# A two-layer decoder kernel: high and low input parts side by side in one tile, one 512-column product in place of two of 256

## The chip, the cores and the metric

The program runs on one core of one Trainium2 chip. The metric is the device time of one execution in microseconds (us); three runs of the kernel before took 2767.17 to 2772.16 us, with a median of 2768.21 us. A core has five engines with a queue each: TensorE (PE in the profile, with its weight loads as PEld), VectorE (DVE), ScalarE (ACT), GpSimd (POOL) and SyncE (SP, which here only issues DMAs). TensorE multiplies a stationary operand of 128x128 (the weights, loaded ahead of each product) by a moving operand of up to 512 columns and adds the result up in PSUM, which has eight banks of 128 x 512 float32.

## The reference, cut to what matters

All arithmetic is float32. 16 meta tokens stand ahead of 256 input tokens, so T = 272; D = 2048.

```
h = concat(meta, x)                                   # 272 x 2048
h = h + rwkv7_time_mix(rms_norm(h))                   # layer 0
h = h + swiglu(rms_norm(h))                           # layer 0, F = 5632
k, v = rms_norm_heads(n @ sb_w_k), n @ sb_w_v         # n = rms_norm(h), 272 tokens
q = rms_norm_heads(rms_norm(h) @ sb_w_q)              # layer 1
h = h + stick_breaking(q, k, v) @ sb_w_o
h = h + (silu(m @ w_gate) * (m @ w_up)) @ w_down      # m = rms_norm(h)
return h[:, 16:]
```

Only the last 256 tokens are returned. From the queries on, layer 1 therefore needs 256 tokens, everything before it 272.

## The kernel before, in words

Activations lie with features on the partitions: a tile is 128 features by 272 or 256 tokens. A projection from 2048 features is 16 steps k over input tiles, for each of its output tiles of 128 features, added up in one PSUM bank.

Float32 accuracy comes from a split. Every weight and every activation is cut into a high part (rounded to the `fp32r` type by ScalarE, `nc.scalar.copy`) and a low part (the rest, by VectorE). A step k is then three `fp32r` products into the same bank: high weights by high input, high weights by low input, low weights by high input (`mm3`, L193 to L201; `mm3k`, L187 to L191; `proj_steps`, L223 to L238, which yields between steps so that other work can be put between them). High and low input parts are two tiles (`split`, L240; `split_gain`, L250).

Weights come from HBM in pieces of 128x1024 (or 128x384 at the end of a w_down row) on SP's queue (`parts`, L154). ScalarE makes `whi` and VectorE `wlo` for four steps at a time (128x512); there are six buffers of each (`NWHL`), so the split can be at most six groups of four steps ahead of TensorE.

The program has these stages: a prologue (first norm, key projection, low-rank inputs), the time mix of 16 head pairs, `wo_first` (output projection), `ffn(0)`, keys and values in `attention`, 16 heads in `attn_head` with the query projection, `sb_w_o`, and `ffn(1)`. `ffn` runs in four quarters: 11 gate tiles and 11 up tiles of 16 steps each, whose scaled product is split into 11 input tiles, then 16 output tiles of `w_down` with 11 steps each. With 256 tokens there are 256 steps of the query projection, 256 of `sb_w_o`, 2 x 44 x 16 = 1408 of gate and up and 4 x 16 x 11 = 704 of down: 2624 steps in all, by three products each.

A finished gate or up bank is read by one VectorE instruction that multiplies it by the norm factor `rs` (L994, L1000; L1087 for queries). A finished `w_down` or `sb_w_o` bank is added to the residual tile `h` by one (L1006, L1076). In `ffn` the banks alternate between two pools of two (`mmbank`, L176), in the heads they come from one pool of two.

The order on each engine's queue is set when the program is built, by a scheduler that follows data dependencies and buffer release. On one engine the instructions run in that order; engines wait for one another by semaphores.

Of the kernel before, what the change touches and what calls it, by code (L numbers as in the profile page):

```python
# [123 lines left out]
class Builder:  # L124
# [68 lines left out]
    def mm3(self, out, w, acts, n0, n1):  # L193
        nc = self.nc
        nk = len(w)
        for k in range(nk):
            wh, wl = w[k]
            xh, xl = acts[k]
            nc.tensor.matmul(out, wh, xh[:, n0:n1], start=k == 0, stop=False)  # L199
            nc.tensor.matmul(out, wh, xl[:, n0:n1], start=False, stop=False)  # L200
            nc.tensor.matmul(out, wl, xh[:, n0:n1], start=False, stop=k == nk - 1)  # L201

    def proj(self, src, acts, nk=NK, m=128, n0=0, n1=T):
        w = self.weights(src, nk, m)
        ps = self.mmbank()
        out = ps[:m, :n1 - n0]
        self.mm3(out, w, acts, n0, n1)
        return out

    def proj_pair(self, srcs, acts, n0=0):  # L210

        parts = [self.parts(src, NK, 128) for src in srcs]
        out = [self.mmbank()[:, :T - n0] for _ in srcs]
        k = 0
        for ws in zip(*parts):
            for i in range(len(ws[0])):
                x = tuple(t[:, n0:] for t in acts[k])
                for o, w in zip(out, ws):
                    self.mm3k(o, w[i], x, k == 0, k == NK - 1)
                k += 1  # L220
        return out

    def proj_steps(self, src, acts, n0=0, step=None):  # L223
        nc = self.nc
        step = step or PSTEP
        w = self.weights(src, NK, 128)
        ps = self.mmbank()
        out = ps[:, :T - n0]
        for k in range(NK):
            wh, wl = w[k]  # L230
            xh, xl = acts[k]
            xh, xl = xh[:, n0:], xl[:, n0:]
            nc.tensor.matmul(out, wh, xh, start=k == 0, stop=False)  # L233
            nc.tensor.matmul(out, wh, xl, start=False, stop=False)  # L234
            nc.tensor.matmul(out, wl, xh, start=False, stop=k == NK - 1)  # L235
            if k % step == step - 1:
                yield 1
        return out  # L238

    def split(self, src, pool, tag):  # L240

        nc = self.nc
        n = src.shape[1]
        hi = pool.tile([128, T], F32R, name="hi", tag=tag)
        lo = pool.tile([128, T], F32R, name="lo", tag=tag)
        nc.scalar.copy(hi[:, :n], src)  # L246
        nc.vector.tensor_tensor(lo[:, :n], src, hi[:, :n].bitcast(F32), ALU.subtract)  # L247
        return hi, lo

    def split_gain(self, src, g, n0, tag):  # L250
        nc = self.nc
        hi = self.xs.tile([128, T], F32R, name="hi", tag=tag)
        lo = self.xs.tile([128, T], F32R, name="lo", tag=tag)
        nc.scalar.activation(hi[:, n0:], src[:, n0:], AF.Copy, scale=g)
        nc.vector.scalar_tensor_tensor(lo[:, n0:], src[:, n0:], g, hi[:, n0:].bitcast(F32),
                                       ALU.mult, ALU.subtract)
        return hi, lo


    def build(self):  # L260
        tc, nc = self.tc, self.nc
        with ExitStack() as ctx:
            cp = ctx.enter_context(tc.tile_pool(name="cp", bufs=1))
            self.xs = ctx.enter_context(tc.tile_pool(name="xs", bufs=32))
# [45 lines left out]
            with ExitStack() as c2:  # L310
# [4 lines left out]
                self.kr = c2.enter_context(tc.tile_pool(name="kr", bufs=32))  # L315
# [15 lines left out]
    def time_mix(self):  # L331
# [3 lines left out]
        hid = self.hid_ctx.enter_context(hid)  # L335
        self.kp = self.hid_ctx.enter_context(tc.tile_pool(name="kp", bufs=NK))
# [25 lines left out]
        for k in range(len(self.o), NK):  # L362
            self.o.append(self.split(self.oraw[k], self.xs, "xs1"))
        self.hid_ctx.close()

    def prologue(self, hid):
# [3 lines left out]
        with ExitStack() as ctx:  # L370
            x0 = ctx.enter_context(tc.tile_pool(name="x0", bufs=32))
            wx = ctx.enter_context(tc.tile_pool(name="wx", bufs=NWX))
            pt = ctx.enter_context(tc.tile_pool(name="pt", bufs=3))
            hn = [self.xs.tile([128, T + 1], F32, name="hn", tag="xs2") for _ in range(NK)]
            xx = [self.xs.tile([128, T], F32, name="xx", tag="xs2") for _ in range(NK)]
# [47 lines left out]
            def mix(i, k, pool, tag):  # L423
                x = pt.tile([128, T], F32, name="xi", tag="tmp")
                mixed(i, k, x)
                return self.split(x, pool, tag)
# [6 lines left out]
            for k in range(NK):  # L433
# [8 lines left out]
                xk.append(mix(2, k, x0, "xs0"))  # L442
# [31 lines left out]
            def rest():  # L474

                for i, name in ((1, "dec_w1"), (4, "a_w1")):
                    ps = self.psd.tile([128, 512], F32, name="lr", tag="sd")[:96, :T]
                    for k in range(NK):
# [3 lines left out]
                        x = self.xs.tile([128, T], F32, name="xi", tag="xs1")  # L482
# [11 lines left out]
                for k in range(KR):  # L494
                    self.xr.append(mix(0, k, self.xs, "xs2"))
                    yield 1
                x = []
                for k in range(NK):
                    x.append(mix(5, k, self.xs, "xs1"))
# [8 lines left out]
                for k in range(NK):  # L508
                    self.xv.append(mix(3, k, self.xs, "xs1"))
                    yield 1  # L510
                for k in range(KR, NK):
                    self.xr.append(mix(0, k, self.xs, "xs2"))
# [407 lines left out]
    def finish_h(self, k, n0, first, gains):  # L920
# [10 lines left out]
        return [self.split_gain(h, self.vec(g, k), n0, t) for g, t in gains]  # L931
# [7 lines left out]
    def wo_head(self):  # L939
# [4 lines left out]
        for k in range(KHEAD):  # L944
            while len(self.oraw) <= k:
                yield 1
            self.o.append(self.split(self.oraw[k], self.xs, "xs1"))
# [11 lines left out]
    def wo_first(self):  # L959
# [3 lines left out]
        for m in range(NK):  # L963
# [11 lines left out]
            acts.append(self.finish_h(m, 0, m == 0, [("g_ffn0", "xs2")])[0])  # L975
# [3 lines left out]
    def ffn(self, layer, n0):  # L979
        nc, a = self.nc, self.a  # L980
        n = T - n0
        gains = [("g_kv", "xs1"), ("g_mix1", "xs2")] if layer == 0 else None
# [205 lines left out]
```

## Time and profile before

| | |
|---|---|
| median of three runs | 2768.21 us |
| profiled execution | 2767.91 us, its span 2766.1 us |
| PE busy | 2713.5 us, 98% of the span |
| DVE busy | 1806.7 us, 65% |
| ACT busy | 1470.2 us, 53% |
| mean granted TensorE clock | 0.995 |
| DMA | 439.86 MB, mean 159 GB/s |

The span is the time from the first to the last recorded instruction; the profiled execution's own time is 1.8 us more. Products overlap in TensorE: a record of a product lasts some 280 ns, while the next one starts 0.12 us after it. What a product costs in a stream is therefore the distance between starts, or a stretch in which PE is busy throughout divided by its count of products, and not the mean duration of a row.

### The profile page before, as it was taken

To read this page: it belongs to the slowest core of one execution; us is meant where nothing else is said; L and a number is where in the kernel's file an instruction comes from. 1 tells how busy PE (TensorE), PEld (TensorE's weight loads), DVE (VectorE), ACT (ScalarE), POOL (GpSimd) and SP (SyncE) were. 2 spreads that over 40 slices of the span, in tenths; PEclk is the share of its full clock that TensorE was granted. 3 is DMA by queue.
4 is the path that set the end of the run, shared out by engine and by line. 5 is a ranking of instruction groups with operands and counts; after the bars stand their busy time and mean duration, and the time that the engine had idled before them with its cause. 6 is when DMAs were issued, how large, how long until landed. Compare 5 with 4: busy or idle time off the path is not lost.

```text
span 2766.1 us, 59131 instructions
## 1 busy us (share of the span) xinstructions
PE 2713.5 (98%) x23486; PEld 2610.8 (94%) x23486; DVE 1806.7 (65%) x3992; ACT 1470.2 (53%) x2901; POOL 1.2 (0%) x11
## 2 busy tenths in 40 slices
PE   6989999999999999999999999999999999999999
PEld 5888888888999999999999999999999999999999
DVE  7677787776765555555556876577666566565665
ACT  7764555554554444444445754577554454454443
POOL 0000000000000000000000000000000000000000
PEclk9999999999999999999999999999999999999999
DMA  5443333331755555555555545533555655655655
GB/s 177 138 137 99 102 95 102 102 95 49 232 174 171 176 180 162 187 174 163 188 174 164 185 161 171 172 108 110 189 183 174 200 183 176 199 184 175 198 175 178
DMA packets 181302, 439.86 MB, mean 159 GB/s; under 512 B 57984, under 2 KB 84000, under 8 KB 181024
## 3 DMA queue, kind: packets, MB, share of 16 engines
q1 hardware_dynamic: 137632, 428.56, 48.0%
q10 hardware_dynamic: 43392, 7.52, 1.4%
q8 instruction: 184, 3.01, 0.5%
q14 instruction: 94, 0.77, 0.1%
HBM read 430.27 MB, written 5.74 MB: 158 GB/s over the span
## 4 chain that ended last, share of the span: by engine, by line
PE 92%; DMA 3%; ACT 2%; DVE 2%; issue 1%; SPq 0%; ACTq 0%; POOLq 0%; POOL 0%; DVEq 0%
PE mm L199 23%; PE mm L200 23%; PE mm L201 23%; PE mm L234 3%; PE mm L233 3%; PE mm L235 3%; DMA raw<-w_k 1%; PE zb L835 1%; PE cb L890 1%; PE yb L818 1%; PE mm L189 1%; PE mm L191 1%; PE mm L190 1%; PE hms L1025 1%; PE wa L844 1%
## 5 line engine op out<-in xcount | busy, mean ns | idle before, releaser
L173 DVE TENSOR_TENSOR wlo<-raw,whi 128x512 fp32r<-128x512 f32 (+1 forms) x1596 | 1079.3, 680 | 712.4 <-ACT whi L172 687.0
L199 PE MATMUL mm<-hi,whi 128*128 128x272 f32 (+1 forms) x5328 | 1523.2, 286 | 1.2 <-DVE h L972 0.9
L172 ACT CAST whi<-raw 128x512 fp32r<-128x512 f32 (+1 forms) x1596 | 972.3, 611 | 1038.6 <-PE mm L200 901.2
L200 PE MATMUL mm<-lo,whi 128*128 128x272 f32 (+1 forms) x5328 | 1520.1, 285 | 0.0
L201 PE MATMUL mm<-hi,wlo 128*128 128x272 f32 (+1 forms) x5328 | 1516.4, 285 | 0.0
L199 PEld LDWEIGHTS mm<-hi,whi 128*128 128x128 f32 x5328 | 1002.3, 188 | 5.5 <-issue 2.6
L201 PEld LDWEIGHTS mm<-hi,wlo 128*128 128x128 f32 x5328 | 1003.9, 188 | 1.4 <-issue 0.9
L200 PEld LDWEIGHTS mm<-lo,whi 128*128 128x128 f32 x5328 | 1004.3, 188 | 0.8
L233 PE MATMUL mm<-hi,whi 128*128 128x272 f32 (+1 forms) x768 | 231.7, 302 | 0.0
L234 PE MATMUL mm<-lo,whi 128*128 128x272 f32 (+1 forms) x768 | 226.2, 295 | 0.0
L235 PE MATMUL mm<-hi,wlo 128*128 128x272 f32 (+1 forms) x768 | 225.5, 294 | 0.0
L234 PEld LDWEIGHTS mm<-lo,whi 128*128 128x128 f32 x768 | 145.4, 189 | 5.4 <-issue 2.3
L233 PEld LDWEIGHTS mm<-hi,whi 128*128 128x128 f32 x768 | 145.3, 189 | 5.1 <-issue 0.7
L235 PEld LDWEIGHTS mm<-hi,wlo 128*128 128x128 f32 x768 | 145.4, 189 | 4.7 <-issue 2.2
L189 PE MATMUL mm<-hi,whi 128*128 128x272 f32 (+1 forms) x208 | 60.9, 307 | 17.7 <-ACT hi L246 17.6
L190 PE MATMUL mm<-lo,whi 128*128 128x272 f32 (+1 forms) x208 | 62.9, 305 | 0.5 <-DVE lo L247 0.4
L191 PE MATMUL mm<-hi,wlo 128*128 128x272 f32 (+1 forms) x208 | 62.9, 306 | 0.0
L189 PEld LDWEIGHTS mm<-hi,whi 128*128 128x128 f32 x208 | 40.1, 200 | 20.8 <-ACT hi L246 19.7
L1006 DVE TENSOR_TENSOR h<-h,mm 128x272 f32<-128x272 f32 (+1 forms) x128 | 54.0, 422 | 6.3 <-PE mm L201 6.3
L994 DVE TENSOR_TENSOR t<-mm,rstd 128x272 f32<-128x272 f32 (+1 forms) x88 | 38.1, 433 | 19.4 <-PE mm L201 15.7
L1000 DVE TENSOR_TENSOR u<-mm,rstd 128x272 f32<-128x272 f32 (+1 forms) x88 | 38.1, 433 | 17.3 <-PE mm L201 15.6
L420 ACT ACTIVATE u<-hn,vecs 128x272 f32<-128x272 f32 x96 | 45.5, 516 | 4.5 <-DVE hn L439 4.5
(270 smaller groups left out, 2187.3 us busy)
## 6 DMA issues: line engine op xcount, KB each, us to landing
raw<-w_gate SPq DMA_DIRECT2D x176, 512.0 KB
raw<-w_up SPq DMA_DIRECT2D x176, 512.0 KB
raw<-w_down SPq DMA_DIRECT2D x128, 512.0 KB
raw<-w_down SPq DMA_DIRECT2D x128, 192.0 KB
raw<-w_k SPq DMA_DIRECT2D x32, 512.0 KB
raw<-w_v SPq DMA_DIRECT2D x32, 512.0 KB
raw<-w_r SPq DMA_DIRECT2D x32, 512.0 KB
raw<-w_o SPq DMA_DIRECT2D x32, 512.0 KB
```

What stands on the lines that cost most here:

```text
L172: nc.scalar.copy(hi, part)
L173: nc.vector.tensor_tensor(lo, part, hi.bitcast(F32), ALU.subtract)
L189: mm(out, w[0], x[0], start=first, stop=False)
L190: mm(out, w[0], x[1], start=False, stop=False)
L191: mm(out, w[1], x[0], start=False, stop=last)
L199: nc.tensor.matmul(out, wh, xh[:, n0:n1], start=k == 0, stop=False)
L200: nc.tensor.matmul(out, wh, xl[:, n0:n1], start=False, stop=False)
L201: nc.tensor.matmul(out, wl, xh[:, n0:n1], start=False, stop=k == nk - 1)
L233: nc.tensor.matmul(out, wh, xh, start=k == 0, stop=False)
L234: nc.tensor.matmul(out, wh, xl, start=False, stop=False)
L235: nc.tensor.matmul(out, wl, xh, start=False, stop=k == NK - 1)
L1006: nc.vector.tensor_tensor(h[:, n0:], h[:, n0:], ps, ALU.add)
```

## The change

An input that 256 tokens wide products will read gets its high and low part in one tile, high in columns 0 to 255 and low in columns 256 to 511 (`pair_tile`). `mm3k` tells the cases apart by the length of the input tuple: with two parts (272 tokens) the three products stay as they were; with a third entry, the whole pair, it issues two products. The first is low weights by high input, 256 columns, into the first half of the bank. The second is high weights by the pair, 512 columns, over the whole bank. The first half of the bank then holds the sum of two of the three partial results, the second half that of high weights by low input, and the two halves must be added when the bank is read.

`scaled` does this for gate, up and query banks: ScalarE copies the second half to SBUF, VectorE adds the first half to the copy, and VectorE multiplies by `rs`. `added` does it for `sb_w_o` and `w_down` banks: two VectorE additions to `h`, one for each half. The tile pools are regrouped to pairs: where 32 single tiles were, there are 16 tiles of twice the width. A key and a value tile share one too. The low-rank inputs `xi` of the prologue, single tiles, now take a pair tile each, 16 in place of 32.

```
     def mm3k(self, out, w, x, first, last):
         mm = self.nc.tensor.matmul
-        mm(out, w[0], x[0], start=first, stop=False)
-        mm(out, w[0], x[1], start=False, stop=False)
-        mm(out, w[1], x[0], start=False, stop=last)
+        if len(x) == 2:
+            mm(out, w[0], x[0], start=first, stop=False)
+            mm(out, w[0], x[1], start=False, stop=False)
+            mm(out, w[1], x[0], start=False, stop=last)
+            return
+        n = x[0].shape[1]
+        mm(out[:, :n], w[1], x[0], start=first, stop=False, skip_group_check=True)
+        mm(out, w[0], x[2], start=False, stop=last, skip_group_check=True)
+
+    def scaled(self, dst, out, rs):
+        V, n = self.nc.vector, dst.shape[1]
+        if out.shape[1] == n:
+            V.tensor_tensor(dst, out, rs, ALU.mult)
+            return
+        c = self.tp.tile([128, SEQ], F32, name="c", tag="half")
+        self.nc.scalar.copy(c, out[:, n:])
+        V.tensor_tensor(dst, out[:, :n], c, ALU.add)
+        V.tensor_tensor(dst, dst, rs, ALU.mult)
+
+    def added(self, h, out):
+        n = h.shape[1]
+        for c in range(0, out.shape[1], n):
+            self.nc.vector.tensor_tensor(h, h, out[:, c:c + n], ALU.add)
...
+    def pair_tile(self, pool, n):
+        t = pool.tile([128, 2 * T], F32R, name="hl", tag="hl")
+        x = (t[:, :n], t[:, n:2 * n])
+        return x if 2 * n > 512 else (*x, t[:, :2 * n])
...
-            self.xs = ctx.enter_context(tc.tile_pool(name="xs", bufs=32))
+            self.xs1 = ctx.enter_context(tc.tile_pool(name="xs1", bufs=NK))
...
-                        x = self.xs.tile([128, T], F32, name="xi", tag="xs1")
+                        x = self.xs1.tile([128, 2 * T], F32, name="xi", tag="hl")[:, :T]
...
-                nc.vector.tensor_tensor(t[:, :n], gp, rs, ALU.mult)
+                self.scaled(t[:, :n], gp, rs)
...
-                nc.vector.tensor_tensor(u[:, :n], up, rs, ALU.mult)
+                self.scaled(u[:, :n], up, rs)
...
-                nc.vector.tensor_tensor(h[:, n0:], h[:, n0:], ps, ALU.add)
+                self.added(h[:, n0:], ps)
```

TensorE's queue at the end of the last w_down tile of `ffn(1)`, before: two steps, each of an input high part `hi` and low part `lo` with the weights `whi` and `wlo` (the figures are buffer numbers).

```order
L199 MATMUL mm_36462<-hi_35513,whi_36458 128x256
L200 MATMUL mm_36462<-lo_35514,whi_36458 128x256
L201 MATMUL mm_36462<-hi_35513,wlo_36459 128x256
L199 MATMUL mm_36462<-hi_35662,whi_36458 128x256
L200 MATMUL mm_36462<-lo_35663,whi_36458 128x256
L201 MATMUL mm_36462<-hi_35662,wlo_36459 128x256
```

The same place after the change, three steps, with the pair tile `hl`; L196 reads its first half, L197 all of it.

```order
L196 MATMUL mm_33999<-hl_33106,wlo_33996 128x256
L197 MATMUL mm_33999<-hl_33106,whi_33995 128x512
L196 MATMUL mm_33999<-hl_33228,wlo_33996 128x256
L197 MATMUL mm_33999<-hl_33228,whi_33995 128x512
L196 MATMUL mm_33999<-hl_33350,wlo_33996 128x256
L197 MATMUL mm_33999<-hl_33350,whi_33995 128x512
```

Two products to a step stand where three stood, and the low weights are needed first.

VectorE's queue where the first quarter of `ffn(1)` goes from up to down, before: `u` is the last scaled up bank, `s` its product with the gate, `lo` the low part of the last down input, `h` the first residual tile, and `wlo` are weight splits for products to come.

```order
L1000 TENSOR_TENSOR u<-mm,rstd 128x256
L173 TENSOR_TENSOR wlo<-raw,whi 128x384
L1001 TENSOR_TENSOR s<-s,u 128x256
L247 TENSOR_TENSOR lo<-s,hi 128x256
L173 TENSOR_TENSOR wlo<-raw,whi 128x512 x2
L1006 TENSOR_TENSOR h<-h,mm 128x256
```

The same place after the change, where `c` is ScalarE's copy of the bank's second half.

```order
L207 TENSOR_TENSOR u<-mm,c 128x256
L173 TENSOR_TENSOR wlo<-raw,whi 128x384
L208 TENSOR_TENSOR u<-u,rstd 128x256
L1014 TENSOR_TENSOR s<-s,u 128x256
L173 TENSOR_TENSOR wlo<-raw,whi 128x512
L255 TENSOR_TENSOR hl<-s,hl 128x256
L173 TENSOR_TENSOR wlo<-raw,whi 128x512
L213 TENSOR_TENSOR h<-h,mm 128x256
L173 TENSOR_TENSOR wlo<-raw,whi 128x384
L213 TENSOR_TENSOR h<-h,mm 128x256
```

One more addition stands ahead of the last low part, a 128x512 weight split too, and the residual tile takes two additions.

ScalarE's queue at this place, before: `s` is the gate, `hi` the high part of the last down input, and the rest are weight casts.

```order
L996 ACTIVATE s<-t 128x256
L172 CAST whi<-raw 128x384
L172 CAST whi<-raw 128x512 x2
L172 CAST whi<-raw 128x384
L246 CAST hi<-s 128x256
L172 CAST whi<-raw 128x512 x2
```

The same after the change, with the copy `c` and the pair tile `hl`.

```order
L1009 ACTIVATE s<-t 128x256
L172 CAST whi<-raw 128x384
L172 CAST whi<-raw 128x512 x2
L206 COPY c<-mm 128x256
L172 CAST whi<-raw 128x384
L172 CAST whi<-raw 128x512
L254 CAST hl<-s 128x256
```

The copy and one more 128x512 weight cast stand ahead of the last high part.

## Rows read from the trace of the kernel before

**Rows 1.** The page: engine totals; the chain that ended last, by engine.

```profile
PE 2713.5 (98%) x23486; PEld 2610.8 (94%) x23486; DVE 1806.7 (65%) x3992; ACT 1470.2 (53%) x2901; POOL 1.2 (0%) x11
...
PE 92%; DMA 3%; ACT 2%; DVE 2%; issue 1%; SPq 0%; ACTq 0%; POOLq 0%; POOL 0%; DVEq 0%
```

**Rows 2.** Stretches: length, busy time (count) of each engine, granted clock, DMA share, GB/s.

```profile
0.00:200.00 200.00, 170.06 (x1152) 148.43 (x1154) 145.85 (x349) 143.71 (x328) 1.19 (x11) 0.98 0.50 156
200.00:700.00 500.00, 481.20 (x5610) 410.45 (x5610) 374.50 (x1347) 273.50 (x646) 0.00 (x0) 0.98 0.33 95
...
1784.00:1931.00 147.00, 147.00 (x1110) 139.28 (x1109) 111.66 (x232) 105.81 (x233) 0.00 (x0) 1.00 0.33 112
1931.00:2014.00 83.00, 82.87 (x700) 82.65 (x699) 58.48 (x108) 47.57 (x91) 0.00 (x0) 1.00 0.56 183
2014.00:2766.00 752.00, 748.95 (x6324) 748.69 (x6323) 449.32 (x783) 360.53 (x629) 0.00 (x0) 1.00 0.57 184
```

**Rows 3.** Waits of all engines: who waited for whom, us in total, times, longest.

```profile
ACT whi L172 <- PE mm L200: 901.2, 1161, 1.7
```

**Rows 4.** Products of 256 columns: count, busy us, mean ns, idle before.

```profile
L199 PE MATMUL mm<-hi,whi 128*128 128x256 f32 x2336 | 657.4, 281 | 0.0
...
L233 PE MATMUL mm<-hi,whi 128*128 128x256 f32 x256 | 75.8, 296 | 0.0
...
L189 PE MATMUL mm<-hi,whi 128*128 128x256 f32 x32 | 9.0, 281 | 0.0
```

**Rows 5.** Stretches of split products alone: 272 columns to 1500, 256 from 2018.

```profile
1100.00:1500.00 400.00, 400.00 (x3184) 400.00 (x3183) 230.54 (x394) 181.27 (x319) 0.00 (x0) 1.00 0.54 174
2100.00:2500.00 400.00, 400.00 (x3378) 400.00 (x3377) 241.44 (x418) 193.43 (x338) 0.00 (x0) 1.00 0.57 186
975.00:1100.00 125.00, 125.00 (x993) 125.00 (x992) 73.14 (x124) 58.30 (x104) 0.00 (x0) 1.00 0.52 172
909.00:970.00 61.00, 61.00 (x492) 61.00 (x491) 34.09 (x60) 26.22 (x45) 0.00 (x0) 1.00 0.57 185
2018.00:2136.00 118.00, 118.00 (x1000) 118.00 (x999) 73.06 (x126) 60.49 (x106) 0.00 (x0) 1.00 0.57 186
2141.00:2200.00 59.00, 59.00 (x503) 59.00 (x502) 33.70 (x61) 26.77 (x47) 0.00 (x0) 1.00 0.61 195
```

**Rows 6.** Timeline of TensorE in a head: start us, us, then the instruction.

```profile
1919.12 0.86 PE L1115 MATMUL lt<-lk,consts 128*128 128x416 f32 x2
1919.82 0.41 PE L1116 MATMUL lt<-lk,consts 128*128 128x144 f32 x2
1920.06 0.30 PE L1118 MATMUL lt<-lk,consts 128*128 128x32 f32 x2
```

**Rows 7.** VectorE and ScalarE groups of 256 columns: count, busy us, mean ns, idle.

```profile
L1006 DVE TENSOR_TENSOR h<-h,mm 128x256 f32<-128x256 f32 x64 | 26.5, 414 | 6.3 <-PE mm L201 6.3
...
L994 DVE TENSOR_TENSOR t<-mm,rstd 128x256 f32<-128x256 f32 x44 | 18.7, 425 | 7.7 <-PE mm L201 5.2 <-PE mm L191 1.0
...
L1131 ACT COPY o<-op 128x256 f32<-128x256 f32 x16 | 6.1, 378 | 1.5 <-PE op L1128 1.5
```

**Rows 8.** Timeline of VectorE from up to down, first quarter of ffn(1).

```profile
2137.81 0.42 DVE L1000 TENSOR_TENSOR u<-mm,rstd 128x256 f32<-128x256 f32 x1
2138.28 0.56 DVE L173 TENSOR_TENSOR wlo<-raw,whi 128x384 fp32r<-128x384 f32 x1
2138.76 0.42 DVE L1001 TENSOR_TENSOR s<-s,u 128x256 f32<-128x256 f32 x1
2139.65 0.42 DVE L247 TENSOR_TENSOR lo<-s,hi 128x256 fp32r<-128x256 f32 x1 [0.47 <-ACT hi L246]
2140.17 0.69 DVE L173 TENSOR_TENSOR wlo<-raw,whi 128x512 fp32r<-128x512 f32 x1
```

**Rows 9.** Timeline of the same place on ScalarE.

```profile
2139.21 0.41 ACT L246 CAST hi<-s 128x256 fp32r<-128x256 f32 x1 [0.96 <-DVE s L1001]
2139.52 0.62 ACT L172 CAST whi<-raw 128x512 fp32r<-128x512 f32 x1
```

**Rows 10.** Timeline of the end of the program.

```profile
2762.67 0.28 PE L201 MATMUL mm<-hi,wlo 128*128 128x256 f32 x1
2762.98 0.42 DVE L1006 TENSOR_TENSOR h<-h,mm 128x256 f32<-128x256 f32 x1 [3.44 <-PE mm L201]
2763.43 0.33 SPq L1014 DMA_DIRECT2D outT<-h  x1
```

More of the change, by code (lines that the diff above doesn't have):

```diff
@@ L188, in mm3k, with proj, proj_pair @@
         mm = self.nc.tensor.matmul
[L189 to L207 removed]
+        if len(x) == 2:
[19 more added lines that the diff above has]
+            self.nc.vector.tensor_tensor(h, h, out[:, c:c + n], ALU.add)
+    def proj(self, src, acts, nk=NK, m=128):
+        w = self.weights(src, nk, m)
+        out = self.mmbank()[:m, :acts[0][-1].shape[1]]
+        for k in range(nk):
+            self.mm3k(out, w[k], acts[k], k == 0, k == nk - 1)
         return out
[L210 removed]
+    def proj_pair(self, srcs, acts):
         parts = [self.parts(src, NK, 128) for src in srcs]
[L213 removed]
+        out = [self.mmbank()[:, :acts[0][-1].shape[1]] for _ in srcs]
         k = 0
@@ L216, in proj_pair, with proj_steps @@
             for i in range(len(ws[0])):
-                x = tuple(t[:, n0:] for t in acts[k])
                 for o, w in zip(out, ws):
-                    self.mm3k(o, w[i], x, k == 0, k == NK - 1)
+                    self.mm3k(o, w[i], acts[k], k == 0, k == NK - 1)
                 k += 1
         return out
-    def proj_steps(self, src, acts, n0=0, step=None):
-        nc = self.nc
+    def proj_steps(self, src, acts, step=None):
         step = step or PSTEP
         w = self.weights(src, NK, 128)
-        ps = self.mmbank()
-        out = ps[:, :T - n0]
+        out = self.mmbank()[:, :acts[0][-1].shape[1]]
         for k in range(NK):
[L230 to L235, printed above, removed]
+            self.mm3k(out, w[k], acts[k], k == 0, k == NK - 1)
             if k % step == step - 1:
@@ L238, in proj_steps, with split, split_gain @@
         return out
-    def split(self, src, pool, tag):
-        nc = self.nc
[L243 to L250, printed above, removed]
-        nc = self.nc
[L252 to L257, printed above, removed]
+    def pair_tile(self, pool, n):
+        t = pool.tile([128, 2 * T], F32R, name="hl", tag="hl")
+        x = (t[:, :n], t[:, n:2 * n])
+        return x if 2 * n > 512 else (*x, t[:, :2 * n])
+    def split(self, src, pool):
+        nc = self.nc
+        x = self.pair_tile(pool, src.shape[1])
+        nc.scalar.copy(x[0], src)
+        nc.vector.tensor_tensor(x[1], src, x[0].bitcast(F32), ALU.subtract)
+        return x
+    def split_gain(self, src, g, pool):
+        nc = self.nc
+        x = self.pair_tile(pool, src.shape[1])
+        nc.scalar.activation(x[0], src, AF.Copy, scale=g)
+        nc.vector.scalar_tensor_tensor(x[1], src, g, x[0].bitcast(F32), ALU.mult, ALU.subtract)
+        return x
     def build(self):
@@ L421, in mixed, with mix @@
                 V.scalar_tensor_tensor(out, hn[k][:, 1:], self.vec(f"om{i}", k), u, ALU.mult, ALU.add)
-            def mix(i, k, pool, tag):
+            def mix(i, k, pool):
                 x = pt.tile([128, T], F32, name="xi", tag="tmp")
                 mixed(i, k, x)
-                return self.split(x, pool, tag)
+                if pool is not self.xs2:
+                    return self.split(x, pool)
+                hi, lo = (pool.tile([128, T], F32R, name=n, tag="s") for n in ("hi", "lo"))
+                A.copy(hi, x)
+                V.tensor_tensor(lo, x, hi.bitcast(F32), ALU.subtract)
+                return hi, lo
             ps = [(self.pmm if m < 2 else self.pfr).tile([128, 512], F32, name="mm",
@@ L946, in wo_head @@
                 yield 1
-            self.o.append(self.split(self.oraw[k], self.xs, "xs1"))
+            self.o.append(self.split(self.oraw[k], self.xs1))
             yield 1
@@ L1132, in attn_head @@
         self.dump("ao", m, o)
-        os[m] = self.split(o, self.xs, "xs1")
+        os[m] = self.split(o, self.xs1)
 def blocks(w, m=128):
```

58 lines of the change are left out of this document (30 added, 28 removed).

## The prediction

> **What bounds the kernel now.** I read the totals first, then the chain, then stretches stage by stage. TensorE is busy for 98% of the span and is 92% of the chain that ended last [rows 1], so a change is worth what it takes off TensorE's queue, or puts between its instructions. By stages the idle time lies in the first 700 us (29.9 and 18.8 us), while from the heads on there is next to none: 0.1 us in the 83 us of the output projection and 3.1 us in the 752 us of the second feed-forward, nearly all of it at the very end [rows 2]. All that the change is about lies in this full part. Over the whole run ScalarE waits 901.2 us for TensorE to release a weight buffer [rows 3]: the weight splits run as far ahead as their six buffers let them, so neither they nor the weight DMAs set the pace. In the second feed-forward VectorE is busy 60% (449.3 of 752) and ScalarE 48% (360.5) [rows 2].
>
> **Products removed.** The steps with 256 tokens are counted in three groups: 2336, 256 and 32, together 2624 [rows 4]. Each loses one of its three instructions, and none of its columns: 3 x 256 before, 256 + 512 after. So everything hangs on what a product costs beyond its columns. In a stretch of nothing but such products one takes 400/3378 = 118.4 ns at 256 columns, and 400/3184 = 125.6 ns at 272 [rows 5]. The granted clock is 1.00 there, the 2.4 GHz level, so 256 columns at one per cycle are 106.7 ns and 272 are 113.3. What is left is 11.7 ns and 12.3 ns. No row has an `fp32r` product of 512 columns; its cost is bounded from both sides:
>
> - If the excess belongs to the instruction (its start, its weight load), the wide product takes 213.3 + 11.7 = 225.0 ns, and a step saves 11.7 ns: 2624 x 11.7 = 30.7 us.
> - If it belongs to the columns, the wide product is twice the narrow one, 236.8 ns, and nothing is saved. A line through the two widths, (125.6 - 118.4)/16 = 0.45 ns a column, is near this end: 118.4 + 256 x 0.45 = 233.6 ns, 3.2 ns a step, 8.4 us.
> - If the excess is a weight load that a long product hides altogether, the wide one takes little over 213.3 ns. The nearest rows are the plain float32 passes of a head: 416 columns start 0.70 us ahead of the next group and are two passes, 350 ns each against 2 x 416/2.4 = 346.7; two passes of 144 columns take 0.24 us, 120 each against 120 [rows 6]. With 3 ns of excess the wide product is 216 ns and a step saves 21 ns, 55 us.
>
> The two widths tell the first two apart weakly, since they differ by 16 columns: 6.67 ns at one column per cycle, 7.40 if all is proportional (118.4/16). The long stretches say 7.2. The matched stages say 61/492 - 59/503 = 124.0 - 117.3 = 6.7 for w_down, and 125/993 - 118/1000 = 125.9 - 118.0 = 7.9 for gate and up [rows 5]. Stages of one width differ by as much as the question does, so I cannot settle it from here. I take the first: the same excess on two widths is what a cost per instruction looks like, and the w_down pair, where the streams are most alike, lies on it. 30.7 us.
>
> One rule of the notes on the chip speaks against this. The Trainium skill, "TensorE: Matmul & The Clock Gate", section "Back-to-back issue gap", gives a warm product N/2.4 + 2.5 ns. By it 256 columns take 109 ns where the trace has 118.4, so it does not hold for these products as it stands; but if its 2.5 ns are all that is fixed here too, the change saves only 2624 x 2.5 = 6.6 us, which is close to the line through the widths and is weighed there.
>
> **Work added behind a bank.** A gate, up or query bank (44 + 44 + 16 = 104) costs ScalarE a copy of 378 ns and VectorE one more instruction of about 425 ns; a w_down or output bank (64 + 16 = 80) costs VectorE one more addition of 414 ns [rows 7]. In the second feed-forward that is 88 x 0.425 + 64 x 0.414 = 64 us on VectorE and 88 x 0.378 = 33 us on ScalarE. VectorE comes to 513 of some 725 us, 71%, ScalarE to 394, 54%. The cover is the lead of the weight splits: six groups of four steps, 6 x 4 x 3 x 118.4 ns = 8.5 us ahead, against about 1.3 us by which the copy and additions hold up the splits queued behind them. Banks come free 0.4 to 0.8 us later, with three others in turn in the feed-forward. I take nothing. Uncovered, it is 104 x (0.378 + 0.425) + 80 x 0.414 = 117 us, the upper end. Going below nothing is excluded: no instruction leaves these two engines.
>
> In the heads the query's way lengthens by the same 0.8 us, with output, score and next-query products of other heads in TensorE's order before anyone needs it; TensorE is busy for 147 of 147 us there [rows 2]. Nothing; at worst 16 x 0.8 = 13 us.
>
> **Low weights first.** The first product of a step now needs `wlo`, which comes after `whi`. With 8.5 us of lead this costs nothing, at worst one split of 0.69 us [rows 8] at a place where the lead is gone.
>
> **The four turns from up to down.** Here the added work has no lead. Before, the last up bank is scaled at 2137.81 and the last low part is done at 2139.65 + 0.42 = 2140.07 [rows 8]. It is needed at the eleventh step of the first down bank, 10 x 3 x 118.4 ns = 3.55 us after the first, about 2141.3: 1.2 us to spare. Now the copy (0.38) and an addition (0.42) come first, and in VectorE's queue a 128x512 split (0.69) stands ahead of the low part, of which 0.47 falls into a wait that is there anyway [rows 8]; ScalarE has one more cast of 0.62 ahead of the high part [rows 9]. So 2140.07 + 0.80 + 0.22 = 2141.1 at the least, and with the cast 2141.7, while the wide steps bring the need forward to 2141.2. That is 0 to 0.5 us late at each of four turns, 0 to 2 us; I take 1.0.
>
> **The end.** The last bank is added and stored: product 2762.67, addition 2762.98 of 0.42, store at 2763.43 [rows 10]. A second addition makes it 0.4 us later.
>
> **Pools.** The low-rank inputs of the prologue get 16 buffers in place of 32, and the scheduler orders the first 700 us slightly otherwise. TensorE's idle time there is 48.7 us [rows 2]; a tenth of that either way, 5 us, is my estimate of what a different order may move. I take nothing.
>
> **Sum.** -30.7 + 1.0 + 0.4 = -29.3 us. The profiled execution took 2767.9 us (span 2766.1 and 1.8 around it) and lies 0.3 below the median of the runs, so 2768.2 - 29.3 = 2739 us. With the excess at 10.6 to 11.7 ns (117.3 and 118.4 less 106.7), 5 us for the pools, and the turns between their ends, this case reaches from 2733 to 2748.
>
> **Rivals.**
>
> *The excess goes with the columns.* The `fp32r` stream takes one column per cycle, the plain passes one in two, and these show almost no excess though each has its weight load too [rows 6]: this speaks for a stream that is simply fed a little too slowly, as do the slopes of 7.2 and 7.9 [rows 5]. Against it is the slope of 6.7, and that a weight load may hide in a slow pass and not in a fast one. By the line through the widths: -8.4 + 1.4 = -7, 2761; between 2756 and 2770.
>
> *The excess is the weight load, and a long product hides it.* For it: one product fewer has a load in its shadow, and the float32 passes hide theirs. Against it: an excess from the load alone should shrink from 256 to 272 columns, and it grew. -55 + 1.4, 2715.
>
> *The hand-over of banks becomes the wait.* Copy, addition and multiplication stand in order on two engines, and the splits are queued behind them; if the lead is used up in every tile, TensorE waits at each bank. For it: VectorE at 71%, and a copy that waits for TensorE at ScalarE's head. Against it: 901 us of waiting on TensorE [rows 3]. It decides from 29 of the 117 us on, a quarter of what is added; with half exposed it is 2739 + 58 = 2797.
>
> **How the numbers follow.** Chances: per instruction 50%, with the columns 33%, hidden load 6%, hand-over 11%. A change under 0.2%, 5.5 us, is about what a measurement of this kernel cannot tell from none. Faster: all of the first and third, 14 of the 33 of the second: 0.70. Slower: 8 of the 11 of the last and 2 of the second: 0.10. The same: 0.20. The range holds the first case and most of the second: 2733 to 2767, leaving out the hidden load, the hand-over and the far end of the columns.
>
> **What would show it.** In the stretch of the second feed-forward, a step (one L196 and one L197) should take 343 ns where three products took 355; 352 says columns, 334 a hidden load. ScalarE should still wait for TensorE at the weight casts. Idle time of TensorE before L196 with VectorE's `wlo` or `hl` as releaser, other than at the turns, would show the last rival. The stages before the heads should take the same time within 5 us; if they don't, the pools count, and the forecast is wrong by that much.

## The result and the profile after

The changed kernel takes 2741.3 us, median of four runs (2737.1 to 2746.7), against 2769.0 for the kernel before: a ratio of 0.9905, interval 0.9891 to 0.9918. That is 27.6 us less, and 2.3 us above the forecast. The span of the profiled execution is 2740.0 us, 26.1 less than before.

The totals and the chain of the page answer to [rows 1].

```profile
PE 2689.3 (98%) x20862; PEld 2475.0 (90%) x20862; DVE 1864.8 (68%) x4176; ACT 1493.5 (55%) x3005; POOL 1.2 (0%) x11
...
PE 91%; DVE 3%; DMA 3%; ACT 2%; ACTq 1%; issue 0%; SPq 0%; DVEq 0%
```

2624 instructions are gone from TensorE, just the number of steps [rows 4], but its share of the span is what it was, and of the chain it has 91% where it had 92%. VectorE and ScalarE have gained 58 and 23 us of work.

The stretches (columns as in [rows 2]): the first 700 us, a stretch of 272 columns, one of 256 and 512, and the whole second feed-forward.

```profile
0.00:200.00 200.00, 171.97 (x1162) 150.72 (x1163) 145.97 (x349) 144.33 (x330) 1.19 (x11) 0.97 0.50 156
200.00:700.00 500.00, 481.23 (x5684) 413.57 (x5684) 386.39 (x1370) 278.96 (x661) 0.00 (x0) 0.98 0.35 101
...
1100.00:1500.00 400.00, 400.00 (x3193) 400.00 (x3192) 232.53 (x399) 182.89 (x322) 0.00 (x0) 1.00 0.56 176
2100.00:2500.00 400.00, 400.00 (x2289) 350.28 (x2289) 270.57 (x510) 209.36 (x392) 0.00 (x0) 1.00 0.59 186
1998.70:2740.00 741.30, 737.39 (x4215) 645.30 (x4214) 496.26 (x935) 383.45 (x717) 0.00 (x0) 1.00 0.59 187
```

The fourth row holds the size that was in dispute. 400/2289 = 174.75 ns a product and two of them to a step are 349.5 ns, where three took 3 x 118.4 = 355.2 [rows 5]. A step saves 5.7 ns in this stretch, and not 11.7. The second row says where the rest came from: in the same 500 us of the first part there are 74 more TensorE instructions than before [rows 2], at the same busy time, in a part where the products did not change.

Each stage ends with a norm whose product `ms` waits for the last residual tile, so its start marks the stage. Of before:

```profile
774.50 0.70 PE L936 MATMUL ms<-sqacc,consts 128*128 128x272 f32 x2
...
1571.53 0.50 PE L936 MATMUL ms<-sqacc,consts 128*128 128x272 f32 x1
...
2013.81 0.45 PE L936 MATMUL ms<-sqacc,consts 128*128 128x256 f32 x1
```

And of after:

```profile
763.46 0.73 PE L949 MATMUL ms<-sqacc,consts 128*128 128x272 f32 x2
...
1558.79 0.50 PE L949 MATMUL ms<-sqacc,consts 128*128 128x272 f32 x1
...
1998.70 0.44 PE L949 MATMUL ms<-sqacc,consts 128*128 128x256 f32 x1
```

| stage | before, us | after, us | difference |
|---|---|---|---|
| prologue and time mix, to the first norm | 774.5 | 763.5 | -11.0 |
| first feed-forward | 797.0 | 795.3 | -1.7 |
| keys and values, heads, output projection | 442.3 | 439.9 | -2.4 |
| second feed-forward, to the end | 752.3 | 741.3 | -11.0 |

So the stages with changed products gave 13.4 us, and 11 came from a part whose products did not change. The first feed-forward has no 512-column product, and still its 1.7 us are not the spread between executions: in eight traces of kernels with pair tiles (the change and the experiments below up to the stride of 14) this stage takes 795.3 us each time. Its inputs, too, lie in pair tiles now; why that makes it shorter is not shown.

### The profile page after: what moved, and what is told of

Its sections match the earlier page's. It is cut to its first block, busy times and chain, and to the rows that moved or that the text cites. A ratio compares the mean times of both kernels' runs of the same rounds, so it can differ in the third digit from the quotient of the medians.

```text
span 2740.0 us, 53870 instructions
## 1 busy us (share of the span) xinstructions
PE 2689.3 (98%) x20862; PEld 2475.0 (90%) x20862; DVE 1864.8 (68%) x4176; ACT 1493.5 (55%) x3005; POOL 1.2 (0%) x11
## 4 chain that ended last, share of the span: by engine, by line
PE 91%; DVE 3%; DMA 3%; ACT 2%; ACTq 1%; issue 0%; SPq 0%; DVEq 0%
PE mm L197 22%; PE mm L191 16%; PE mm L193 16%; PE mm L192 15%; PE mm L196 11%; DMA raw<-w_k 1%; PE cb L903 1%; PE yb L831 1%; PE rm L871 1%; PE zb L848 1%; PE hms L1038 1%; PE cb L896 1%; PE z L1115 1%; DVE G L721 0%; PE ba L715 0%
## 5 line engine op out<-in xcount | busy, mean ns | idle before, releaser
L191 PE MATMUL mm<-hl,whi 128*128 128x272 f32 x3424 | 996.9, 292 | 19.4 <-ACT hl L254 18.5
L193 PE MATMUL mm<-hl,wlo 128*128 128x272 f32 x3424 | 995.9, 291 | 0.0
L192 PE MATMUL mm<-hl,whi 128*128 128x272 f32 x3424 | 991.4, 290 | 0.4 <-DVE hl L255 0.3
L197 PE MATMUL mm<-hl,whi 128*128 128x512 f32 x2624 | 919.8, 395 | 0.0
L196 PE MATMUL mm<-hl,wlo 128*128 128x256 f32 x2624 | 740.6, 282 | 0.0
L191 PEld LDWEIGHTS mm<-hl,whi 128*128 128x128 f32 x3424 | 645.8, 189 | 27.7 <-ACT hl L254 20.5
L192 PEld LDWEIGHTS mm<-hl,whi 128*128 128x128 f32 x3424 | 652.6, 191 | 4.2 <-DVE hl L255 1.3
L193 PEld LDWEIGHTS mm<-hl,wlo 128*128 128x128 f32 x3424 | 647.9, 189 | 4.8 <-issue 1.8
L197 PEld LDWEIGHTS mm<-hl,whi 128*128 128x128 f32 x2624 | 492.5, 188 | 112.7
L196 PEld LDWEIGHTS mm<-hl,wlo 128*128 128x128 f32 x2624 | 494.3, 188 | 0.6
L213 DVE TENSOR_TENSOR h<-h,mm 128x256 f32<-128x256 f32 (+1 forms) x224 | 93.9, 420 | 6.6 <-PE mm L197 6.0
L193 PEld LDWEIGHTS mm<-hi,wlo 128*128 128x128 f32 x256 | 48.8, 191 | 2.9 <-issue 2.4
L191 PEld LDWEIGHTS mm<-hi,whi 128*128 128x128 f32 x256 | 48.9, 191 | 2.4
L192 PEld LDWEIGHTS mm<-lo,whi 128*128 128x128 f32 x256 | 48.9, 191 | 1.0
```

What stands on the lines that cost most here:

```text
L196: mm(out[:, :n], w[1], x[0], start=first, stop=False, skip_group_check=True)
L197: mm(out, w[0], x[2], start=False, stop=last, skip_group_check=True)
L213: self.nc.vector.tensor_tensor(h, h, out[:, c:c + n], ALU.add)
```

## The experiments

Each ratio and gain below is against executions of the kernel before that were made beside the experiment's (medians 2767.3 to 2769.3 us).

The first question is which part of the change earned which part of the time. Theory: the wide product earns what it saves at about 5 ns a step, and the pair tiles of the pool `xs1`, which holds the low-rank inputs, earn the first 11 us by the order that they lead the scheduler to. Rival: all of it is the products, and the first part differs by chance.

**Pools alone.** All pools and pair tiles of the change, but three products to a step:

```diff
-        x = (t[:, :n], t[:, n:2 * n])
-        return x if 2 * n > 512 else (*x, t[:, :2 * n])
+        return t[:, :n], t[:, n:2 * n]
```

> The pair tiles and all pools of the change, but three products of 256 columns to a step and the old single read of a bank. Theory of the prediction (the gain is one instruction less per step, pools move nothing): no gain, 2764 to 2774 us, the norm product of the first feed-forward still starts at about 774 us. Theory of the new trace (about 11 us come from another order of TensorE's queue in the time mix, which the pair tiles bring about): 2756 to 2759 us, that product at 763 to 764 us, and the second feed-forward as long as before, 752 us.

Measured: 2757.6, ratio 0.9964 (0.9951 to 0.9976), so 9.7 us faster with not one product fewer. The first `ms` and the one that ends the first feed-forward, then a stretch of the second feed-forward and the whole of it:

```profile
762.66 0.50 PE L948 MATMUL ms<-sqacc,consts 128*128 128x272 f32 x1
1557.99 0.50 PE L948 MATMUL ms<-sqacc,consts 128*128 128x272 f32 x1
```

```profile
2100.00:2500.00 400.00, 400.00 (x3369) 400.00 (x3368) 241.21 (x417) 192.57 (x337) 0.00 (x0) 1.00 0.57 184
2000.76:2755.80 755.04, 751.90 (x6324) 751.64 (x6324) 450.35 (x783) 359.91 (x629) 0.00 (x0) 1.00 0.57 183
```

The first norm comes 11.8 us earlier than before, and a product takes 118.7 ns, where it took 118.4. What I had set at nothing, the pools, is worth more than a third of the gain. One thing I had not expected: the pair tiles alone make the second feed-forward 2.8 us longer (755.1 against 752.3), as they make the first 1.7 us shorter. From there the wide product saves 13.8 us in the second feed-forward, and not only 11.0.

**Products alone.** The wide products, with all of the pool `xs1`, the low-rank inputs among it, in single tiles (the output projection, which uses the same pool, keeps three products; 2368 of the 2624 steps are wide). TensorE's order in the first part is then that of before, product by product in the two traces.

```diff
+        if pool is self.xs1:
+            hi, lo = (pool.tile([128, T], F32R, name=x, tag="hl") for x in ("hi", "lo"))
+            return hi[:, :n], lo[:, :n]
...
-            self.xs1 = ctx.enter_context(tc.tile_pool(name="xs1", bufs=NK))
+            self.xs1 = ctx.enter_context(tc.tile_pool(name="xs1", bufs=2 * NK))
```

> The change, but the pool xs1 keeps high and low parts in single tiles as before, 32 of them; the output projection of the heads then stays at three products, so 2368 of 2624 steps are wide. TensorE's order up to the first feed-forward is then that of the kernel before. Theory of the prediction: 90% of the gain stays, 2742 to 2745 us. Theory of the new trace (a step saves about 5 ns, the rest is the order): 2368 x 4.9 ns = 11.6 us, 2756 to 2759 us, the norm product at about 774 us and the second feed-forward at 741 us.

Measured: 2756.0, ratio 0.9955 (0.9941 to 0.9969), 11.3 us faster. First `ms` and stretch:

```profile
780.54 0.50 PE L952 MATMUL ms<-sqacc,consts 128*128 128x272 f32 x1
```

```profile
2100.00:2500.00 400.00, 400.00 (x2289) 350.17 (x2288) 270.48 (x508) 210.38 (x394) 0.00 (x0) 1.00 0.60 188
```

The step is that of after, 349.5 ns, and the gain of the first part is gone with the order: this execution's `ms` is even 6 us later than before. (It was the slowest of its five, 4.4 above their median, and the time that the granted clock cost, added up in slices of 15 us up to `ms` (a slice times the share that was not granted), is 20.7 us here, 13.5 in before, 13.8 in after and 11.7 in the run with the pools alone. Less that time, the first `ms` stands at 759.8 here, 761.0 in before, 749.7 in after and 751.0 with the pools alone: the two with single tiles and the two with pairs lie some 10 us apart. In the four other traces with TensorE's order of after it starts at 760.6 to 763.5.) The two halves add up to 21.0 us of the 27.6. The 256 steps left out are 1.4 more, and 2.8 is what the wide product saves beyond its 11.0 once the tiles are pairs; the rest is within the intervals of three comparisons, some 3.5 us to either side of each.

**What a product costs by its width.** Other widths: 384 columns with the high weights and 128 with the low ones in the query, gate, up and output steps, 448 and 192 in the down steps, so 512 and 640 columns to a step. Parts of the sums are left out (fewer columns of the low weights' product, and only the first half of each bank is read).

```diff
-        mm(out[:, :n], w[1], x[0], start=first, stop=False, skip_group_check=True)
-        mm(out, w[0], x[2], start=False, stop=last, skip_group_check=True)
+        a, b = self.widths
+        mm(out[:, :b], w[0], x[2][:, :b], start=first, stop=False, skip_group_check=True)
+        mm(out[:, :a], w[1], x[0][:, :a], start=False, stop=last, skip_group_check=True)
```

> The two products of a step get other widths: 384 columns with the high weights and 128 with the low ones for query, gate, up and output banks, 448 and 192 for w_down; banks are read once, first half only. It leaves out the columns beyond. A cost per instruction (11.7 ns over 2.4 GHz): 65, 92, 172 and 198 ns for 128, 192, 384 and 448 columns. A cost that goes with the columns (line through 118.1 ns at 256 and 232.3 at 512, that is 4 ns and 0.446 ns a column): 61, 90, 175 and 204 ns.

Measured: 2617.9 us, one execution. A step of 512 columns takes 283 ns and one of 640 takes 314, which is neither theory's sum (237 or 236, and 290 or 294; so near each other that only single products could have told them apart). The timelines of the weight loads and of the products:

```profile
2049.93 0.19 PEld L197 LDWEIGHTS mm<-hl,whi 128*128 128x128 f32 x1
2050.04 0.19 PEld L198 LDWEIGHTS mm<-hl,wlo 128*128 128x128 f32 x1
2050.21 0.19 PEld L197 LDWEIGHTS mm<-hl,whi 128*128 128x128 f32 x1
2050.32 0.19 PEld L198 LDWEIGHTS mm<-hl,wlo 128*128 128x128 f32 x1
```

```profile
2049.70 0.39 PE L197 MATMUL mm<-hl,whi 128*128 128x384 f32 x1
2049.93 0.22 PE L198 MATMUL mm<-hl,wlo 128*128 128x128 f32 x1
2049.98 0.39 PE L197 MATMUL mm<-hl,whi 128*128 128x384 f32 x1
2050.21 0.22 PE L198 MATMUL mm<-hl,wlo 128*128 128x128 f32 x1
```

The loads follow one another by 0.11 and 0.17 us in turn: the narrow product starts 0.05 us ahead of the next wide one, but no load here starts less than 0.11 us after another. So I read it that a product of 128 columns holds its place for a load's time, and that the experiment for this reason did not measure what it was made for. By the line through two widths that the experiment on the operands' type gives below, 384 columns are 174.7 ns and 448 are 203.4; what is left of the steps is 108 ns for 128 columns and 111 for 192, nearly the same for both, and over the stage the loads of the low weights start 108 ns after those of the high ones. This division of a step is a reading and not shown: the starts of the products themselves have the narrow one at 58 and 88 ns and the wide one at 226 for either width. Measured are the steps, which are longer than their columns on that line (235 and 292).

**Contention.** Rival for the excess over one column per cycle: VectorE, ScalarE and the weight DMAs share the memory with TensorE's operands. In the second feed-forward one set of weights serves all products, so no weight is brought in, cast or split there (all other weights of that stage are left out).

```diff
-                    gp = self.proj(a[f"w_gate{layer}"][q * FB + j], hx)
+                    gp = self.proj(a[f"w_gate{layer}"][q * FB + j], hx, w=wq)
```

> In the second feed-forward all products use one set of 16 weight tiles, loaded and split once: no weight DMAs, no weight casts and splits there (it computes with the wrong weights). If the excess over 2.4 GHz is other engines and DMAs taking SBUF away from TensorE: products of 256 and 512 columns fall to about 109 and 216 ns, a step to 325, the stage from 741 to about 690 us. If it belongs to TensorE's own streams: 118 and 232 ns, 350 a step, 740 us.

Measured: 2736.4 us, one execution, and this stretch (columns as before; the last number is GB/s):

```profile
2100.00:2500.00 400.00, 400.00 (x2291) 350.42 (x2291) 90.02 (x213) 37.35 (x95) 0.00 (x0) 1.00 0.00 1
```

With VectorE at a third of its work, ScalarE at less than a fifth and the DMAs at 1 GB/s, a step takes 349.2 ns. Over the stage the starts are 117.8 and 230.9 ns apart, where after has 117.5 and 232.3: of the 30 ns by which a step exceeds one column per cycle, about 1 goes. The excess does not come from the neighbours, and the rival falls.

**The type of the operands.** Second feed-forward with the split parts in `bfloat16`, columns and instructions the same (the parts carry fewer bits).

```diff
+                if self.bfw:
+                    hi, lo = hi.bitcast(BF16)[:, :n], lo.bitcast(BF16)[:, :n]
...
+        self.bfw = layer == 1
...
+            self.bfa = True
```

> In the second feed-forward all split parts, weights and inputs, are bfloat16 in place of fp32r, with the same columns, products and engines (the result loses accuracy). If the excess belongs to streams of four bytes an element: products of about 109 and 216 ns, a step of 325, the stage 686 to 700 us where the change has 741. If it belongs to products of any type (their accumulation in PSUM, their instructions): 118 and 232 ns, 350 a step, 740 us.

Measured: 2688.2 us, one execution, and on TensorE:

```profile
2299.82 0.27 PE L204 MATMUL mm<-hl,wlo 128*128 128x256 bf16 x1
2299.93 0.38 PE L205 MATMUL mm<-hl,whi 128*128 128x512 bf16 x1
2300.15 0.27 PE L204 MATMUL mm<-hl,wlo 128*128 128x256 bf16 x1
2300.26 0.38 PE L205 MATMUL mm<-hl,whi 128*128 128x512 bf16 x1
```

The starts over the stage are 109.2 and 215.8 ns apart, 2.5 ns a product above one column per cycle (106.7 and 213.3). The Trainium skill, "TensorE: Matmul & The Clock Gate", section "Back-to-back issue gap", gives N/2.4 + 2.5 ns for a single warm product, which is 109.2 and 215.8, and about 131 ns for 512 columns in a sustained stream: in this stream of `bfloat16` the trace agrees with the first and not with the second, and the measurement decides. In `fp32r` the same stage of the changed kernel has 117.5 and 232.3 ns; three starts of it:

```profile
2300.20 0.28 PE L196 MATMUL mm<-hl,wlo 128*128 128x256 f32 x1
2300.32 0.40 PE L197 MATMUL mm<-hl,whi 128*128 128x512 f32 x1
2300.55 0.28 PE L196 MATMUL mm<-hl,wlo 128*128 128x256 f32 x1
```

The line through these two widths is (232.3 - 117.5)/256 = 0.448 ns a column and 2.7 ns a product; through the run without neighbours it is 0.442 and 4.7. So the fixed part is known to some 2 ns only, and by the column the stream is 6 to 7.6% slower than that of `bfloat16`. Most of the excess goes with the columns, which joining two products keeps. Whether it is the bytes of an operand or the arithmetic that slows the stream is not shown.

A join should by these lines save 2.7 to 4.7 ns a step, and 5.2 over the stage were measured. What is missing lies in the products before: the starts of the three are 118.9, 118.5 and 117.7 ns apart (high weights by high input, high by low, low by high), so the two that were joined took about 1 ns each more than the third. With the pair tiles alone they are 116.6, 120.1 and 119.8. An `fp32r` product of the same columns thus takes a few ns more or less with the tiles that it reads; the cause is not shown.

**The hand-over of banks.** No copy and no second addition; only the first half of each bank is read (the second half, the low input parts with the high weights, is left out).

```diff
-        c = self.tp.tile([128, SEQ], F32, name="c", tag="half")
-        self.nc.scalar.copy(c, out[:, n:])
-        V.tensor_tensor(dst, out[:, :n], c, ALU.add)
-        V.tensor_tensor(dst, dst, rs, ALU.mult)
+        V.tensor_tensor(dst, out[:, :n], rs, ALU.mult)
```

> The change with its banks read once, the first half only: no copy and no added addition (it leaves the second half's partial result out). The prediction holds the added work for hidden but for 1.0 us at the turns and 0.4 at the end: 0.8 to 1.4 us under the change, 2738 to 2741 us. The rival of the hand-over would have it 10 us or more faster, under 2731 us. The new trace shows no late product at a turn, which says 0.4 us.

Measured: 2738.6, ratio 0.9887 (0.9870 to 0.9904), where after has 0.9905: all the added work on two engines is gone, and the medians are 2.7 us apart, less than either interval. In the stretch (rows as above) VectorE's load falls back to that of before, and TensorE's rate does not change:

```profile
2100.00:2500.00 400.00, 400.00 (x2290) 350.17 (x2289) 244.95 (x425) 196.02 (x343) 0.00 (x0) 1.00 0.60 186
```

The two traces say it more closely. The last `ms` and the start of the last product in this run:

```profile
1998.26 0.48 PE L945 MATMUL ms<-sqacc,consts 128*128 128x256 f32 x1
...
2735.54 0.39 PE L197 MATMUL mm<-hl,whi 128*128 128x512 f32 x1
```

That is 737.3 us, where after has 737.0 (1998.70 to 2735.70). The hand-over is hidden, as forecast.

**Why the new order of the time mix is shorter.** A count suggested itself: TensorE goes from the products of 272 columns (and the transposes `tb` and `tv`, taken with them) to the small ones of the head pairs and back 482 times before and 458 times after. Theory: each change of kind costs it something. Two strides of the same planner give other counts: 14 instead of 13 gives 428, and 12 gives 504.

```diff
-STRIDE = 13
+STRIDE = 14
```

> The change with a distance of 14 in place of 13 steps between the head pairs of the time mix: TensorE's queue there goes 428 times from split products to small products or back, where the change does so 458 times and the kernel before 482 times. If these alternations set the time mix (24 fewer went with 11 us less): 13 us less, norm product at about 750 us, 2727 us in all. If an alternation costs only the 0.1 us that its row shows: 3 us less, 2738 us. If it is the waits in the chain of a pair and not the count: anything from 5 us less to 10 us more.

> The same with a distance of 12: 504 alternations. By the count: 21 us more, norm product at about 784 us. By 0.1 us each: 5 us more, 768 us. By waits: no rule, and not the opposite of the distance of 14.

Measured with 14: 2742.0, ratio 0.9897 (0.9878 to 0.9916), no different from after with 30 changes fewer. With 12: 2783.6, one execution. Their first `ms`:

```profile
764.28 0.50 PE L949 MATMUL ms<-sqacc,consts 128*128 128x272 f32 x1
```

```profile
805.12 0.50 PE L949 MATMUL ms<-sqacc,consts 128*128 128x272 f32 x1
```

This count explains neither. What the stride of 12 adds is partly clock (21.9 us up to `ms` against 13.8 in after) and partly waiting: TensorE's idle time up to `ms` is 66.8 us against 46.8, and this is its longest entry among TensorE's waits between 177 and 740 us (us, times, longest), ahead of the same entry of after between 177 and 700:

```profile
PE yb L831 <- DMA Tt<-s: 18.7, 11, 7.1
```

```profile
PE yb L831 <- DMA Tt<-s: 2.8, 1, 2.8
```

So the theory falls for the count that I had made, but not for every count: by the split products alone (those into `mm`, `gp`, `zw` and `za`) against all others the traces have 535 changes before, 497 after, 499 with 14 and 561 with 12, which is also the order of the first `ms`. No run tells such a cost from the waits that change with it. What stays: of the 11.0 us, 2.5 are idle time of TensorE and 8.5 are busy time of the same 7350 products. The stretch up to the first `ms`, of before and of after:

```profile
0.00:774.50 774.50, 725.16 (x7351) 632.63 (x7351) 573.05 (x1794) 460.16 (x1055) 1.19 (x11) 0.98 0.41 122
```

```profile
0.00:763.46 763.46, 716.66 (x7350) 627.59 (x7350) 574.33 (x1794) 458.19 (x1055) 1.19 (x11) 0.98 0.41 123
```

The granted clock is the same, 0.98. From 177 us on, taking each product's distance to the next start, the split products `mm` take 6 us less in sum, `wa` 4, `b`, `zb` and `yb` 3 each, while `rm` takes 5 more, `vc` and `gp` 2 each. It is spread, and which neighbour in the order causes it is open.

**A version that beats both.** `bfloat16` parts in every projection from the first feed-forward on; the edit is that of the second feed-forward with the switches set earlier. A high and a low part then carry fewer bits of an input or a weight together.

```diff
+        self.bfa = True
...
+        self.bfw = True
```

> The change, with bfloat16 split parts in every projection from the first feed-forward to the end (a split then carries fewer bits than with fp32r). A product of 272 columns should fall from 125.5 to 115.8 ns, of 256 from 118 to 109.2, of 512 from 232.3 to 215.8. First feed-forward 2112 x 3 x 9.7 ns = 61 us less, keys and values 512 x 3 x 9.7 = 15 us, query and output 512 x 25 = 13 us, second feed-forward 52 us: about 2600 us. If VectorE or the weight DMAs become the bound somewhere: 2620 to 2690 us, with TensorE waiting for weight splits.

Measured: 2603.0, ratio 0.9398 (0.9380 to 0.9416). In the stretch of 272 columns a product takes 600/5183 = 115.8 ns, where it had 125.6 [rows 5]:

```profile
800.00:1400.00 600.00, 600.00 (x5183) 506.81 (x5181) 372.38 (x642) 294.59 (x519) 0.00 (x0) 1.00 0.61 190
```

## Why the prediction was right, and where it was not

The time and the sign came out right. That the time did is luck: two terms of the sum were wrong, and their errors cancelled.

**The step that failed: "I take the first: the same excess on two widths is what a cost per instruction looks like."** The wide product takes 232.3 ns (or 349.5 - 118.4 = 231.1 by the stretch of before), not 225.0. 2624 steps by 11.7 ns were to give 30.7 us; measured are 5.7 ns in the long stretch and, over the stage, 11.0 us for 2107 steps, 5.2 ns. With the 2.4 us of the stages between, that is 13.4 us. The mechanism of the first rival, an excess that goes with the columns, is the one the runs bear out: the line through 256 and 272 columns gave 233.6, and only its saving was a little small, 3.2 ns a step against 5.2. The reading that misled was a difference of 0.5 ns between two excesses, 11.7 and 12.3, taken as equal. Over 16 columns the slower stream would add just that: 16 x (0.448 - 0.417) = 0.5 ns. The contrary evidence stood in the prediction, in the slopes of 7.2 and 7.9 ns [rows 5].

**"Pools. [...] I take nothing."** The bound of 5 us was an estimate from idle time. The order gave 11.0 us in the trace, and 9.7 us by the run with the pools alone, mostly out of time in which TensorE counted as busy, which an estimate by idle time cannot see. The prediction's own condition ("if they don't, the pools count, and the forecast is wrong by that much") came true; the wide product's mistake happened to be the opposite.

**Work behind a bank, and low weights first: nothing.** Right. The run without it has the same step time in the second feed-forward, and its last product starts no earlier after the last `ms`. ScalarE still waits for TensorE at the weight casts, as said; two of its waits in the second feed-forward (us, times, longest), the second at the new copy:

```profile
ACT whi L172 <- PE mm L197: 226.3, 352, 1.7
ACT c L206 <- PE mm L197: 64.7, 87, 1.7
```

VectorE comes to 496.3 of 741 us there, 67% where 71% was worked out, ScalarE to 383.5, 52% against 54%: the added instructions were counted at full length, and in part they overlap their neighbours, as the rows below show (0.56 us from 2121.38 on, the next from 2121.85).

**The four turns: 1.0.** They cost nothing that the traces show. The copy and what follows it on VectorE, first quarter (the places of [rows 8] after):

```profile
2120.56 0.37 ACT L206 COPY c<-mm 128x256 f32<-128x256 f32 x1 [0.72 <-PE mm L197]
```

```profile
2120.96 0.42 DVE L207 TENSOR_TENSOR u<-mm,c 128x256 f32<-128x256 f32 x1 [0.40 <-ACT c L206]
2121.38 0.56 DVE L173 TENSOR_TENSOR wlo<-raw,whi 128x384 fp32r<-128x384 f32 x1
2121.85 0.42 DVE L208 TENSOR_TENSOR u<-u,rstd 128x256 f32<-128x256 f32 x1
2122.30 0.42 DVE L1014 TENSOR_TENSOR s<-s,u 128x256 f32<-128x256 f32 x1
2122.66 0.69 DVE L173 TENSOR_TENSOR wlo<-raw,whi 128x512 fp32r<-128x512 f32 x1
2123.26 0.42 DVE L255 TENSOR_TENSOR hl<-s,hl 128x256 fp32r<-128x256 f32 x1
```

From the start of the copy to the end of the last low part it takes 3.1 us, inside the 3.5 us (ten steps of 349.5 ns) that the first ten steps of the next bank last, and TensorE shows no wait there.

**The end: 0.4.** It is 0.6, from 2736.13 + 0.87 - 2735.70 = 1.30 where [rows 10] had 0.73 for the same way from the last product's start to the last addition's end; 0.45 of that is the addition, the rest the longer last product.

```profile
2735.70 0.39 PE L197 MATMUL mm<-hl,whi 128*128 128x512 f32 x1
2736.13 0.87 DVE L213 TENSOR_TENSOR h<-h,mm 128x256 f32<-128x256 f32 x2 [2.97 <-PE mm L197]
2737.03 0.33 SPq L1027 DMA_DIRECT2D outT<-h  x1
```

The sum as measured: -13.4 for products (end and turns in it), -11.0 for the order, -1.7 for the first feed-forward, where the products are the same and the tiles are not, together -26.1.

**The other rivals.** The hidden load would have shown 334 ns a step and is out. The hand-over as a wait is out by the run that removes it.

## What to carry to other kernels

Joining two products that share weights saves only what a product costs beyond its columns; read that from two widths that lie far apart, and if the rows offer only near ones, give the slope as much weight as the excess. Whatever changes the size or the sharing of tiles also changes the scheduler's order elsewhere: compare the order of every stage, and price it by the busy time that the order may hold as well as by the idle time. When a total agrees, check the terms: here the right total was the sum of two errors.

## What was not expected of the hardware

- A product of `fp32r` operands streams at 0.448 ns a column with 2.7 ns on top (117.5 ns at 256, 232.3 at 512), in `bfloat16` at 0.4167 with 2.5 (109.2 and 215.8), at the same granted clock of 1.00. Without weight traffic the `fp32r` products still take 117.8 and 230.9. With `bfloat16` in the projections from the first feed-forward on, the whole run is 5% shorter than after (2603.0 against 2741.3).
- Weight loads of 128 columns in `fp32r` followed one another by no less than 107 ns in the run with other widths. Narrow products gained little: a step of 384 and 128 columns took 283 ns and one of 448 and 192 took 314, where the columns alone would give 235 and 292 on the line above. The Trainium skill, "TensorE: Matmul & The Clock Gate", section "LDWEIGHTS", gives P/1.2, which is 107 ns for 128: the trace agrees.
- `fp32r` products of the same width take other times in other tiles: the second feed-forward with three products to a step 752.3 us from single tiles and 755.1 from pairs, the first 797.0 and 795.3. In the second feed-forward of the changed kernel, `fp32r` products of 256 columns start 112 to 122 ns ahead of the next one, and in `bfloat16` 108 to 111. The cause is open.
- The same 7350 products of the time mix cost TensorE 8.5 us less of busy time in another order. The cause is open.
